# Low parts of some down weights by an accumulating transfer in a two-layer encoder trunk

## The chip, the cores and the metric

The kernel runs on one NeuronCore of a Trainium2 chip. The metric is the device time of one execution in microseconds, as the median of several runs. Every profile here is of one execution. The engines are TensorE (PE in the profile; PEld are its weight loads), VectorE (DVE), ScalarE (ACT), GpSimd (POOL) and SyncE (SP, which issues the DMAs).

## What is computed

The reference is a trunk of two layers on 256 tokens of width 1024, in float32:

```python
for i in range(DEPTH):                                  # DEPTH = 2, ALPHA = (2 * DEPTH) ** 0.25
    x = layer_norm(ALPHA * x + 0.5 * swiglu(x, ffn1_w_gate[i], ffn1_w_up[i], ffn1_w_down[i]), ...)
    proj = x @ (rwkv_w_in[0] if i == 0 else sb_w_in[0])
    mix = rwkv7_mix(...) if i == 0 else stick_breaking_mix(...)
    heads = concatenate([mix, memory_attention(mq, mem_k, mem_v)], axis=-1)
    x = layer_norm(ALPHA * x + heads @ w_out[i], ...)
    x = layer_norm(ALPHA * x + 0.5 * swiglu(x, ffn2_w_gate[i], ffn2_w_up[i], ffn2_w_down[i]), ...)

def swiglu(x, w_gate, w_up, w_down):                    # 1024 x 2816, 1024 x 2816, 2816 x 1024
    return (jax.nn.silu(x @ w_gate) * (x @ w_up)) @ w_down
```

The first layer's mixer is a recurrence over 256 steps (chunks of 64), the second's is a causal attention of its own kind. The weights are read once from device memory; they make up nearly all of the 301 MB that the profile counts as read.

## The kernel before

**Matmuls in three parts.** TensorE multiplies in a reduced float format (float32r). To keep float32 accuracy, each operand is split into a high part, rounded to that format, and a low part, the rest. A product is three matmuls that add up in PSUM (`mm3`, line 664): high by high, high by low, low by high. The tokens are two halves of 128 rows. A matmul has 128 rows of weights as its one operand, 128 tokens as its other, and 512 columns of output.

**Pieces of weights.** `piece` (line 636) handles 128 x 1024 weights at a time, 512 KB. SP loads them into a slot `raw`. ScalarE copies `raw` to a slot `hi`, which rounds it (line 647). VectorE subtracts `hi` from `raw` into a slot `lo` (line 649). There are 10 slots `raw` and 9 each of `hi` and `lo`, 4096 bytes on each partition. A `raw` slot is free for the next load when the subtraction has read it.

**Feed-forward blocks.** `ffn_block` (line 774) does 256 of the 2816 hidden columns: four pieces of gate and up weights (`gu`) and two of down weights (`dn`). For the given halves, it makes 24 matmuls of 512 columns per half into one PSUM bank, then the gating on ScalarE and VectorE, then a transpose, a split into high and low, and 12 matmuls per half with the down weights into the half's accumulators. The down part of a block is put behind the gate and up part of the next one (`blocks`, line 1421).

**Stages.** While one half goes through a layer's mixer, which consists of many short steps on all engines that wait for each other, the other half goes through feed-forward blocks of its own: `solo(1, ...)`, the first blocks of the layer's first feed-forward for half 1, beside the mixer of half 0, and `solo(0, ...)`, the first blocks of the second feed-forward for half 0, beside the mixer of half 1. In layer 0 these are 5 and 9 blocks (`LAGS`, line 47). The remaining blocks serve both halves. A layer norm on VectorE stands between the stages.

**Who sets the order.** The program is first only recorded: each operation becomes an `Op` with a cost (`price`, line 291), its dependencies, and the slots it opens and closes. `order` (line 346) then places the operations one after another on five engine clocks, by the earliest possible start and a priority. SP's loads, the high parts and the low parts each keep a sequence of their own (`in_turn`). `improve` (line 542) repeats that 24 times with priorities from due times that are counted back from the end (`latest`), with a random shake of fixed seed, and keeps the plan with the earliest end. `issue` (line 573) writes the instructions in that order. Each engine's order is thus fixed at build time, all instructions stand under line 599 in the profile, and a change of one cost or one operation changes the order of the whole program. Small copies (`copy`, line 209) may go to ScalarE or VectorE, as the planner finds.

GpSimd does nothing but 14 memsets. All DMAs are issued by SP.

Of the kernel before, what the change touches and what calls it, by code (L numbers as in the profile page):

```python
# [58 lines left out]
BESIDE = (True, False)  # L59


BLK = 16
_LEVELS = [16, 32]

# [66 lines left out]
class Plan:  # L131
# [33 lines left out]
    def slot(self, pool, shape, dtype, tag, name, bufs):  # L165

        handle = bass.PSumTensorHandle if pool.name == "ps" else bass.SBTensorHandle
        tile = handle(name, list(shape), dtype)[:]
        key = pool.name, tag
        self.tag_of[name] = key  # L170
        self.pools[key] = pool
        self.slots[key] = max(bufs, self.slots.get(key, 0))
        self.size[key] = max(int(np.prod(shape[1:])), self.size.get(key, 0))
        return tile

    def region(self, ap):
# [114 lines left out]
    def price(self, o, method, aps, a, k):  # L291
        free = lambda x: int(np.prod([n for _, n in x.ap[1:]])) if len(x.ap) > 1 else 1
        sb = lambda x: x.space != PSUM
        o.func, o.port, o.kb = None, False, 0.0
        outs = [x for x, w in aps if w]
        ins = [x for x, w in aps if not w]
        n = max(free(x) for x, _ in aps)
        far = 0.9 * n * any(len(x.ap) > 1 and x.ap[-1][0] >= 16 and x.ap[-1][1] > 1 for x, _ in aps)
        if o.eng == "PE":
            out, st, mv = a[0], a[1], a[2]  # L300
            cols, m, rows = free(mv), free(st), st.ap[0][1]
            half = lambda x, n: range(x.offset // x.ap[0][0] // 64, (x.offset // x.ap[0][0] + n - 1) // 64 + 1)
            o.mode, o.round = (rows <= 64, m <= 64), st.dtype == F32R
            if method == "transpose":
                took, o.lag = 110.0, 175.0
            elif st.dtype == F32R:
                took, o.lag = max(cols / 2.4, m / 1.2) + 13.3, 180.0
            else:
                took, o.lag = 2 * max(cols / 1.2, m / 1.2 + 4), 200.0
                if rows <= 64 and cols > 128:  # L310
                    took *= 1.25
            o.parts.append((took, [(r, c) for r in half(st, rows) for c in half(out, m)], min(rows, P) / P))
        elif o.eng == "ACT":
            fun = a[2] if len(a) > 2 else k["func"]
            o.func = {AF.Exp: "Exp", AF.Tanh: "Tanh", AF.Sigmoid: "Sigmoid", AF.Ln: "Ln", AF.Silu: "Silu"}.get(fun)
            ptr = sum(isinstance(k.get(x), bass.AP) for x in ("scale", "bias"))
            o.took = 95.0 + 0.845 * n + far + 93.0 * ptr + (92.0 if "accum_out" in k else 0.0)
            o.lag = 95.0
        elif o.eng == "DVE":
            two = sum(sb(x) and free(x) == n for x in ins) > 1  # L320
            big = [x for x in aps if free(x[0]) > 1]
            fast = method in ("tensor_copy", "tensor_scalar") and all(sb(x) for x, _ in aps)
            o.port = two or fast
            ptr = sum(free(x) == 1 and n > 1 for x in ins)
            o.took = 75.0 + n / (1.92 if fast else 0.96) + far + 58.0 * (ptr > 0) * (n > 1)
            if sum(free(x) == 1 for x in ins) > 2:
                o.took += 115.0
            if method == "transpose":
                o.took = 75.0 + n / 0.96 + 60.0
            o.lag = 83.0  # L330
        elif o.eng == "POOL":
            o.port = method != "memset"
            rate = 0.9 if method == "memset" else 2.2 if method in ("tensor_tensor", "tensor_sub", "tensor_mul") else 1.4
            if n <= 70 and method != "tensor_copy":
                rate, base = 1.5, 210.0
            else:
                base = 130.0
            if method == "tensor_copy" and n < 32:
                base = 500.0
            o.took, o.lag = base + rate * n, 78.0  # L340
        else:
            o.kb = max(int(np.prod(x.shape)) for x, w in aps) * 4 / 1024
            o.fine = min(x.shape[-1] for x, w in aps) <= 256
            o.took, o.lag = 400.0, 0.0

    def order(self, given=()):
# [50 lines left out]
        while done < len(ops):  # L397
# [68 lines left out]
            if e == "SP":  # L466
                landed = max(t + LAND + 400.0 * o.fine, landed) + o.kb * 1024 / 330.0
                o.end = landed
            for n in o.opens:
                b = self.buffer[n] = heapq.heappop(free[self.tag_of[n]])[1]  # L470
                self.reuse += [(j, o.i) for j in held.get((self.tag_of[n], b), ())]
                held[self.tag_of[n], b] = set(self.seen[n]["ops"])
# [130 lines left out]
def kernel(ctx, tc, const, x, mem, f1g, f1u, f1d, f2g, f2u, f2d, ln_g, ln_b, w_out, w_mem_kv,  # L603
# [29 lines left out]
        return slice(hf * P, (hf + 1) * P)  # L633


    def piece(shape, *srcs):

        n = int(np.prod(shape))
        hi = new(wp, [P, D], F32R, "hi", "hi", NHI)[:, :n]
        lo = new(wp, [P, D], F32R, "lo", "lo", NLO)[:, :n]  # L640
        raw = new(wp, [P, D], F32, "raw", "raw", NRAW)[:, :n]
        v = lambda t: t.rearrange("p (a b) -> p a b", a=shape[0]) if len(shape) == 2 else t
        m = shape[-1] // len(srcs)
        made = [nc.sync.dma_start(v(raw)[..., i * m:(i + 1) * m], src) for i, src in enumerate(srcs)]
        for o in made:
            nc.in_turn("load", o)
        first = nc.scalar.activation(hi, raw, AF.Copy)
        nc.in_turn("hi", first)
        made.append(nc.vector.tensor_sub(lo, raw, hi.bitcast(F32)))
        nc.in_turn("lo", made[-1])  # L650
        nc.lead.update((o.i, first.i) for o in made + [first])
        return v(hi), v(lo)

# [117 lines left out]
            turn_x(hf)  # L771


    def ffn_block(w, c, halves, beside):
        gv, uv, dv = (m.rearrange("(k p) c -> p k c", p=P) for m in w)
        fs = slice(c * FC, (c + 1) * FC)
        gu = [piece((2, 2 * FC), *(v[:, 2 * g:2 * g + 2, fs] for v in (gv, uv))) for g in range(4)]
        dn = [piece((D,), dv[:, 2 * c + q, :]) for q in range(2)]
        state = {}
        for hf in halves:  # L780
            if todo[hf] == 0:
# [636 lines left out]
        seq += [((i + 0.49) / len(shared), c, range(NHALF)) for i, c in enumerate(shared)]  # L1418
        return [(c, h) for _, c, h in sorted(seq, key=lambda t: t[0])]

    def blocks(w, seq, beside=False):
        waiting = []
        for c, halves in seq:
            hidden = yield from ffn_block(w, c, halves, beside)
            yield from chain(*waiting)
            waiting = hidden()
        yield from chain(*waiting)

    def solo(hf, cs):
        return [(c, [hf]) for c in cs]  # L1430
# [5 lines left out]
    for i in range(DEPTH):  # L1436
        mixer, steps = ((rwkv, RW), (stick, SB))[i % 2]
        last = i == DEPTH - 1
        lag1, lag2 = LAGS[i]
        w = f1g[i], f1u[i], f1d[i]  # L1440
        if i == 0:
            seq = spread((0, range(lag1)), range(lag1, NFC))
            run(blocks(w, seq[:2]))
            nc.in_turn("load", nc.sync.dma_start(cst[:, P:], const[:, P:]))
            run(blocks(w, seq[2:4]))
            rwkv_constants()
            gb = ln_g[i, 0], ln_b[i, 0]
            run(blocks(w, seq[4:]))
        else:
            run(blocks(w, solo(0, range(FIRST))))  # L1450
            gb = ln_g[i, 0], ln_b[i, 0]
            run(blocks(w, spread((0, range(FIRST, lag1)), range(lag1, NFC))))
        norm(0, 2.0 * ALPHA, 4.0 * LN_EPS, gb)
        mixed = []
        run(blocks(w, solo(1, range(HEAD)), BESIDE[0]))
        if i == 0:
            run(memory_kv())
        alternate(chain_steps(mixer(0, mixed)), blocks(w, solo(1, range(HEAD, lag1)), True), steps)
        norm(1, 2.0 * ALPHA, 4.0 * LN_EPS, gb)
        gb = ln_g[i, 1], ln_b[i, 1]  # L1460
        w = f2g[i], f2u[i], f2d[i]
        second = chain_steps(mixer(1, mixed))
        for _ in range(PRE[i]):
            next(second)
        run(chain_steps(mixed_out(0, mixed[0], w_out[i])))
        norm(0, ALPHA, LN_EPS, gb)
        alternate(second, blocks(w, solo(0, range(lag2 - HOLD[i])), True), steps)
        run(chain_steps(mixed_out(1, mixed[1], w_out[i])), blocks(w, solo(0, range(lag2 - HOLD[i], lag2)), BESIDE[1]))
        norm(1, ALPHA, LN_EPS, gb)
        gb = ln_g[i, 2], ln_b[i, 2]  # L1470
        run(blocks(w, spread((1, range(TAIL[i], lag2)), range(lag2, NFC))))
        norm(0, 2.0 * ALPHA, 4.0 * LN_EPS, gb, last)
        run(blocks(w, solo(1, range(TAIL[i]))))
        norm(1, 2.0 * ALPHA, 4.0 * LN_EPS, gb, last)
# [25 lines left out]
```

## Time and profile before

| what | us |
|---|---|
| median of 3 runs | 1103.34 (1101.57 to 1103.51) |
| profiled execution, first to last instruction | 1099.8 |
| TensorE busy | 1062.8 |
| VectorE busy | 928.8 |
| ScalarE busy | 751.6 |
| GpSimd busy | 2.7 |

The profile's page knows the span of the profiled execution alone; the runs' times are 3.5 us above it at the median, which is what lies around the first and the last instruction. Names such as `lo_14r` are slots: the name that the slot's first tile had. One slot serves many pieces after each other. `hi`, `lo` and `raw` are the slots of the weights; `xTh` and `xTl` are the high and low parts of the tokens; `hT` those of the gated hidden values; `ps` are PSUM banks. A matmul of 512 columns stands with a duration of 0.39 us, and the next one starts 0.23 us after it, since matmuls overlap; so TensorE's busy time isn't a measure of how much it could still take. The DMA share is the part of the time in which the 16 DMA engines had packets under way, on average.

### The profile page before, as it was taken

Reading aid. Unit: us, or ns where it says so; the run is one execution under the profiler, and the core shown is the slowest. Engines: PE = TensorE matmul, PEld = TensorE weight load, DVE = VectorE, ACT = ScalarE, POOL = GpSimd, SP = SyncE. Lnnn points to the kernel's source line nnn. Section 1 sums busy time; section 2 is a strip of 40 time slices with the busy share of each in tenths; the row PEclk is TensorE's granted clock in tenths of the full one; section 3 lists DMA queues with packets and bytes.
Section 4 is the critical chain, followed back from the end, with each engine's and each line's share of the span. In section 5 each row is a group of like instructions: output and inputs, shape, how many; then the busy total and the mean of one; then the engine's idle time right before and its main releaser. Section 6 shows DMA issues by size and latency. Waiting matters only on the chain.

```text
span 1099.8 us, 17711 instructions
## 1 busy us (share of the span) xinstructions
PE 1062.8 (97%) x6265; PEld 861.4 (78%) x6265; DVE 928.8 (84%) x1312; ACT 751.6 (68%) x1021; POOL 2.7 (0%) x14
## 2 busy tenths in 40 slices
PE   7999999998799999999999999999999999999996
PEld 6878887876678787778888888888877877888885
DVE  6567677999999999998889965649899989987777
ACT  7466566987369786676668654547898898866652
POOL 0000000000000000000000000000000000000000
PEclk9999999999989999999999999999999999999998
DMA  9499758866679587799989976657987987998781
GB/s 344 149 363 378 262 203 291 295 216 204 190 226 336 179 288 251 256 297 369 323 271 362 352 244 212 206 195 258 392 292 269 349 284 266 376 379 292 264 289 59
DMA packets 212250, 303.30 MB, mean 276 GB/s; under 512 B 13844, under 2 KB 159424, under 8 KB 212162
## 3 DMA queue, kind: packets, MB, share of 16 engines
q1 hardware_dynamic: 212162, 302.18, 80.5%
q8 instruction: 49, 0.80, 0.3%
q14 instruction: 39, 0.32, 0.1%
HBM read 301.08 MB, written 1.05 MB: 275 GB/s over the span
## 4 chain that ended last, share of the span: by engine, by line
PE 79%; DVE 13%; DMA 3%; issue 2%; ACT 2%; SPq 0%; DVEq 0%; ACTq 0%
PE ps_30r L599 25%; PE ps_29r L599 24%; PE ps_26r L599 6%; PE ps_25r L599 6%; PE ps_28r L599 6%; PE ps_27r L599 6%; PE ps_2r L599 3%; PE ps_3r L599 3%; DVE x L599 1%; DMA raw_45r<-in_ffn_w_up_dram 1%; DVE lo_44r L599 1%; DVE lb_498r L599 1%; DMA raw_21r<-in_ffn_w_up_dram 1%; DVE lo_20r L599 1%; DVE lo_17r L599 1%
## 5 line engine op out<-in xcount | busy, mean ns | idle before, releaser
L599 ACT ACTIVATE h_32r<-ps_30r 128x256 f32<-128x256 f32 (+1 forms) x35 | 15.1, 431 | 23.1 <-PE ps_30r L599 23.1
L599 ACT ACTIVATE h_31r<-ps_29r 128x256 f32<-128x256 f32 (+1 forms) x34 | 14.5, 426 | 18.5 <-PE ps_29r L599 18.5
L599 PE MATMUL ps_30r<-hi_22r,xTh 128*128 128x512 f32 x64 | 26.3, 410 | 0.0
L599 PE MATMUL ps_30r<-hi_22r,xTl 128*128 128x512 f32 x64 | 25.0, 391 | 0.0
L599 PE MATMUL ps_30r<-lo_23r,xTh 128*128 128x512 f32 x64 | 25.0, 391 | 0.0
L599 PE MATMUL ps_30r<-hi_10r,xTh 128*128 128x512 f32 (+1 forms) x58 | 23.0, 397 | 0.0
L599 PE MATMUL ps_29r<-hi_16r,xTh 128*128 128x512 f32 x56 | 22.4, 401 | 0.0
L599 PE MATMUL ps_29r<-hi_40r,xTh 128*128 128x512 f32 (+1 forms) x56 | 22.4, 401 | 0.0
L599 PE MATMUL ps_30r<-hi_10r,xTl 128*128 128x512 f32 (+1 forms) x58 | 22.3, 385 | 0.0
L599 PE MATMUL ps_30r<-lo_11r,xTh 128*128 128x512 f32 (+1 forms) x58 | 22.2, 383 | 0.0
L599 PE MATMUL ps_29r<-hi_16r,xTl 128*128 128x512 f32 x56 | 21.9, 391 | 0.0
L599 PE MATMUL ps_29r<-lo_17r,xTh 128*128 128x512 f32 x56 | 21.9, 391 | 0.0
L599 PE MATMUL ps_29r<-hi_40r,xTl 128*128 128x512 f32 (+1 forms) x56 | 21.5, 384 | 0.0
L599 PE MATMUL ps_29r<-lo_41r,xTh 128*128 128x512 f32 (+1 forms) x56 | 21.5, 383 | 0.0
L599 PE MATMUL ps_30r<-hi_13r,xTh 128*128 128x512 f32 x52 | 21.4, 412 | 0.0
L599 PE MATMUL ps_30r<-hi_7r,xTh 128*128 128x512 f32 x52 | 21.2, 408 | 0.0
L599 PE MATMUL ps_30r<-lo_14r,xTh 128*128 128x512 f32 x52 | 20.5, 394 | 0.4 <-DVE lo_14r L599 0.4
L599 PE MATMUL ps_2r<-cst,x 128*128 128x128 f32 x48 | 8.9, 316 | 12.2 <-DVE x L599 6.7
L599 PE MATMUL ps_29r<-lo_44r,xTh 128*128 128x512 f32 x50 | 19.7, 395 | 0.9 <-DVE lo_44r L599 0.8
L599 PE MATMUL ps_30r<-lo_17r,xTh 128*128 128x512 f32 x50 | 19.7, 393 | 0.8 <-DVE lo_17r L599 0.8
L599 PE MATMUL ps_30r<-hi_7r,xTl 128*128 128x512 f32 x52 | 20.4, 392 | 0.0
L599 PE MATMUL ps_30r<-hi_13r,xTl 128*128 128x512 f32 x52 | 20.4, 392 | 0.0
(1923 smaller groups left out, 4044.8 us busy)
## 6 DMA issues: line engine op xcount, KB each, us to landing
raw_45r<-in_ffn_w_down_dram SPq DMA_DIRECT2D x17, 512.0 KB, 4.1
raw_24r<-in_ffn_w_down_dram SPq DMA_DIRECT2D x16, 512.0 KB, 4.6
raw_15r<-in_ffn_w_gate_dram SPq DMA_DIRECT2D x30, 256.0 KB, 4.6
raw_15r<-in_ffn_w_up_dram SPq DMA_DIRECT2D x30, 256.0 KB, 5.6
raw_21r<-in_ffn_w_down_dram SPq DMA_DIRECT2D x15, 512.0 KB, 6.3
raw_39r<-in_ffn_w_gate_dram SPq DMA_DIRECT2D x30, 256.0 KB, 4.8
raw_39r<-in_ffn_w_up_dram SPq DMA_DIRECT2D x30, 256.0 KB, 4.9
raw_42r<-in_ffn_w_down_dram SPq DMA_DIRECT2D x15, 512.0 KB, 5.1
```

What stands on the lines that cost most here:

```text
L599: fn(*[at(x) for x in a], **{n: at(x) for n, x in k.items()})
```

## The change

For some pieces the low part is made in another way: `lo` is not a subtraction on VectorE. ScalarE copies `raw` a second time with a scale of -1 into `lo`, which makes the negated high part there. Then GpSimd issues a DMA from `raw` to `lo` that adds what it reads to what stands in its destination. So `lo` holds `raw` minus the high part when the DMA has landed. TensorE's matmuls on `lo` wait for that DMA, and `raw` is in use until then.

`ADDED` names the pieces: numbers 4 and 5 of a block, the two of the down weights, in the `solo` blocks of layer 0 (first and second feed-forward). That is 2 x (5 + 9) = 28 pieces. In layer 1 there are none. The planner gets a price for the new operation (1 us on GpSimd, 4 us until it has landed, and its bytes on the count of transfers). Slots' sizes are rounded up to 16 elements, 64 bytes.

```diff
+ADDED = (((4, 5), (4, 5)), ((), ()))
+LINE = 16
...
-        self.size[key] = max(int(np.prod(shape[1:])), self.size.get(key, 0))
+        self.size[key] = max(-(-int(np.prod(shape[1:])) // LINE) * LINE, self.size.get(key, 0))
...
+        elif o.eng == "POOL" and method == "dma_start":
+            o.kb = max(int(np.prod(x.shape)) for x, w in aps) * 4 / 1024
+            o.took, o.lag = 1000.0, 4000.0
...
+            elif o.kb:
+                landed += o.kb * 1024 / 330.0
...
-    def piece(shape, *srcs):
+    def piece(shape, *srcs, added=False):
...
-        made.append(nc.vector.tensor_sub(lo, raw, hi.bitcast(F32)))
-        nc.in_turn("lo", made[-1])
+        if added:
+            made.append(nc.scalar.activation(lo, raw, AF.Copy, scale=-1.0))
+            nc.in_turn("lo", made[-1])
+            made.append(nc.gpsimd.dma_start(lo.bitcast(F32), raw, accum_op=ALU.add))
+        else:
+            made.append(nc.vector.tensor_sub(lo, raw, hi.bitcast(F32)))
+            nc.in_turn("lo", made[-1])
...
-        gu = [piece((2, 2 * FC), *(v[:, 2 * g:2 * g + 2, fs] for v in (gv, uv))) for g in range(4)]
-        dn = [piece((D,), dv[:, 2 * c + q, :]) for q in range(2)]
+        gu = [piece((2, 2 * FC), *(v[:, 2 * g:2 * g + 2, fs] for v in (gv, uv)), added=g in added) for g in range(4)]
+        dn = [piece((D,), dv[:, 2 * c + q, :], added=4 + q in added) for q in range(2)]
```

`blocks` hands `ADDED[i][0]` to the `solo` blocks of the first feed-forward and `ADDED[i][1]` to those of the second; the other calls hand over nothing.

More of the change, by code (lines that the diff above doesn't have):

```diff
@@ L771, in norm, with ffn_block @@
             turn_x(hf)
-    def ffn_block(w, c, halves, beside):
+    def ffn_block(w, c, halves, beside, added):
         gv, uv, dv = (m.rearrange("(k p) c -> p k c", p=P) for m in w)
         fs = slice(c * FC, (c + 1) * FC)
-        gu = [piece((2, 2 * FC), *(v[:, 2 * g:2 * g + 2, fs] for v in (gv, uv))) for g in range(4)]
-        dn = [piece((D,), dv[:, 2 * c + q, :]) for q in range(2)]
+        gu = [piece((2, 2 * FC), *(v[:, 2 * g:2 * g + 2, fs] for v in (gv, uv)), added=g in added) for g in range(4)]
+        dn = [piece((D,), dv[:, 2 * c + q, :], added=4 + q in added) for q in range(2)]
         state = {}
@@ L1419, in spread, with blocks @@
         return [(c, h) for _, c, h in sorted(seq, key=lambda t: t[0])]
-    def blocks(w, seq, beside=False):
+    def blocks(w, seq, beside=False, added=()):
         waiting = []
         for c, halves in seq:
-            hidden = yield from ffn_block(w, c, halves, beside)
+            hidden = yield from ffn_block(w, c, halves, beside, added)
             yield from chain(*waiting)
@@ L1454 @@
         mixed = []
-        run(blocks(w, solo(1, range(HEAD)), BESIDE[0]))
+        run(blocks(w, solo(1, range(HEAD)), BESIDE[0], ADDED[i][0]))
         if i == 0:
             run(memory_kv())
-        alternate(chain_steps(mixer(0, mixed)), blocks(w, solo(1, range(HEAD, lag1)), True), steps)
+        alternate(chain_steps(mixer(0, mixed)), blocks(w, solo(1, range(HEAD, lag1)), True, ADDED[i][0]), steps)
         norm(1, 2.0 * ALPHA, 4.0 * LN_EPS, gb)
@@ L1466 @@
         norm(0, ALPHA, LN_EPS, gb)
-        alternate(second, blocks(w, solo(0, range(lag2 - HOLD[i])), True), steps)
-        run(chain_steps(mixed_out(1, mixed[1], w_out[i])), blocks(w, solo(0, range(lag2 - HOLD[i], lag2)), BESIDE[1]))
+        alternate(second, blocks(w, solo(0, range(lag2 - HOLD[i])), True, ADDED[i][1]), steps)
+        run(chain_steps(mixed_out(1, mixed[1], w_out[i])), blocks(w, solo(0, range(lag2 - HOLD[i], lag2)), BESIDE[1], ADDED[i][1]))
         norm(1, ALPHA, LN_EPS, gb)
```

## The prediction

> **What bounds the kernel now.** I read the page first, then the stretches, then the chain inside the first layer. The page's totals, two rows of its slices and its chain by engine:
>
> ```profile
> span 1099.8 us, 17711 instructions
> PE 1062.8 (97%) x6265; PEld 861.4 (78%) x6265; DVE 928.8 (84%) x1312; ACT 751.6 (68%) x1021; POOL 2.7 (0%) x14
> ...
> DVE  6567677999999999998889965649899989987777
> ACT  7466566987369786676668654547898898866652
> ...
> PE 79%; DVE 13%; DMA 3%; issue 2%; ACT 2%; SPq 0%; DVEq 0%; ACTq 0%
> ```
>
> As a whole TensorE is the limit. But busy shares are averages over stages: VectorE's row stands at 9 from the eighth slice to the nineteenth (a slice is 27.5 us), and the chain gives VectorE 13% of the span, 143 us. The stretches (length, then PE, PEld, DVE, ACT, POOL busy, granted clock, DMA share, GB/s) place this:
>
> ```profile
> 158.00:303.00 145.00, 133.98 (x1297) 109.00 (x1295) 136.38 (x242) 100.92 (x164) 0.84 (x4) 0.97 0.73 245
> 303.00:488.00 185.00, 180.05 (x1481) 144.94 (x1482) 182.70 (x310) 138.89 (x202) 0.21 (x1) 0.99 0.79 258
> 200.00:488.00 288.00, 272.45 (x2579) 220.45 (x2578) 282.82 (x505) 208.21 (x320) 1.05 (x5) 0.98 0.74 243
> 488.00:750.00 262.00, 262.00 (x1188) 215.24 (x1187) 198.50 (x244) 157.35 (x196) 0.00 (x0) 1.00 0.83 279
> ```
>
> From 200 to 488 us, the first layer's mixer beside feed-forward blocks, VectorE is busy 282.8 of 288 us (98%), ScalarE 208.2 (72%), GpSimd 1. From 488 on TensorE is busy throughout and VectorE 76%. So VectorE's work has a price in the first layer's mixer stages and none behind them. All 28 pieces that the change touches lie there: 10 with subtractions at 158 to 270 us (five blocks of the first feed-forward), 18 at 336 to 480 us (nine of the second).
>
> **What the change removes.** 28 subtractions on VectorE. One group of such rows, and three rows in a row, which give the pitch:
>
> ```profile
> L599 DVE TENSOR_TENSOR lo_11r<-raw_45r,hi_10r 128x1024 fp32r<-128x1024 f32 x4 | 4.9, 1218 | 3.5 <-ACT hi_10r L599 3.5
> ```
> ```profile
> 409.72 1.22 DVE L599 TENSOR_TENSOR lo_14r<-raw_21r,hi_13r 128x1024 fp32r<-128x1024 f32 x1
> 410.85 1.22 DVE L599 TENSOR_TENSOR lo_23r<-raw_9r,hi_22r 128x1024 fp32r<-128x1024 f32 x1
> 411.99 0.71 DVE L599 STREAM_TRANSPOSE Tt_358r<-Y_369r 128x512 f32<-128x512 f32 x1
> ```
>
> One lasts 1.22 us, but the next operation starts 1.13 us after it: it holds the engine 1.13 us. 28 x 1.13 = 31.6 us of VectorE.
>
> **What it adds on ScalarE.** 28 copies with a scale, next to the plain copy that makes the high part:
>
> ```profile
> 419.00 1.04 ACT L599 ACTIVATE hi_40r<-raw_39r 128x1024 fp32r<-128x1024 f32 x1
> 419.95 1.04 ACT L599 ACTIVATE hi_16r<-raw_15r 128x1024 fp32r<-128x1024 f32 x1
> ```
>
> The pitch is 0.95 us. A constant scale is not shown for this size; the plain copy is the nearest row, so 28 x 0.95 = 26.6 us. ScalarE has 80 us idle in 200 to 488, but not everywhere. I therefore work out the gain by windows, those in which the chain runs over VectorE, where subtractions like these stand on it:
>
> ```profile
> 230.00:271.00 41.00, 37.12 (x348) 28.41 (x347) 40.55 (x75) 32.04 (x61) 0.00 (x0) 0.96 0.64 216
> 346.00:416.00 70.00, 67.33 (x524) 53.48 (x523) 69.78 (x130) 57.91 (x96) 0.21 (x1) 1.00 0.75 242
> 441.00:488.00 47.00, 45.44 (x296) 36.37 (x293) 45.84 (x80) 33.58 (x40) 0.00 (x0) 1.00 0.82 266
> ```
> ```profile
> 237.49 1.14 DVE lo_11r L599
> 238.63 1.14 DVE lo_14r L599
> 239.76 0.68 DVE lo_38r L599
> ```
>
> - 230 to 271 holds six removed subtractions (two are the chain rows above). VectorE falls to 40.55 - 6.78 = 33.8, ScalarE rises to 32.04 + 5.7 = 37.7 and is now the fuller: at most 41 - 37.7 = 3.3 us.
> - 346 to 416 holds eight: VectorE 69.78 - 9.04 = 60.7, ScalarE 57.91 + 7.6 = 65.5: at most 4.5 us.
> - 441 to 488 holds four: VectorE 45.84 - 4.52 = 41.3, ScalarE 33.58 + 3.8 = 37.4: VectorE stays the fuller, 4.5 us.
>
> Together 12.3 us. The other ten (four at 158 to 198, two at 336, four at 422 to 438) lie where the chain runs mostly over matmuls; I count their 11.3 us of VectorE at nothing. What hides them is TensorE; if that cover goes, they are gain as well. This is also a sum over the old windows. The planner places everything anew and may spread ScalarE's load to its idle places, hence the larger rival below.
>
> **The transfer itself.** No row of before shows an accumulating transfer, nor one from GpSimd. Nearest rows: weight loads of the same 512 KB, a load's issue on SP, GpSimd's longest operation:
>
> ```profile
> raw_45r<-in_ffn_w_down_dram SPq DMA_DIRECT2D x17, 512.0 KB, 4.1
> ...
> raw_21r<-in_ffn_w_down_dram SPq DMA_DIRECT2D x15, 512.0 KB, 6.3
> ```
> ```profile
> 411.00 0.37 SPq L599 DMA_DIRECT2D raw_21r<-in_ffn_w_gate_dram  x1
> ```
> ```profile
> L599 POOL MEMSET S_110r<- 128x768 f32 x1 | 0.7, 737 | 0.1
> ```
>
> Bounds: 0.37 + 4.1 = 4.5 us, and, if reading two operands and writing one takes three loads' time, 0.74 + 3 x 6.3 = 19.6 us. I take 0.74 + 6.3 = 7.0, one slow load, because the bytes that land are the same. What waits for it is the first matmul on that low part. How long did the low parts lie ready before? Smallest and largest case of the 28 (the subtraction, then the first matmul that reads its result):
>
> ```profile
> 157.99 1.22 DVE L599 TENSOR_TENSOR lo_14r<-raw_15r,hi_13r 128x1024 fp32r<-128x1024 f32 x1
> ```
> ```profile
> 165.75 0.40 PE L599 MATMUL ps_27r<-lo_14r,hT_35r 128*128 128x512 f32 x1
> ```
> ```profile
> 336.50 1.22 DVE L599 TENSOR_TENSOR lo_17r<-raw_18r,hi_16r 128x1024 fp32r<-128x1024 f32 x1
> ```
> ```profile
> 377.24 0.40 PE L599 MATMUL ps_26r<-lo_17r,hT_833r 128*128 128x512 f32 x1
> ```
>
> 6.5 and 39.5 us; down weights are used only after the next block's gate and up products. In the new order, the matmuls between the last one that the negated copy depends on and the first use add up, by the pitches of before, to 7.0 and 7.3 us in one pair of pieces, to 11 to 15 in eight others, and to over 16 in the rest. That is TensorE's work alone, its idle time comes on top. At 7 us nothing waits. At 19.6 most would.
>
> The transfer also keeps its raw slot until it has landed, and loads wait for raw slots:
>
> ```profile
> SPq L599 <- DVE lo_41r L599: 23.7, 11, 10.3
> ```
> ```profile
> q1 hardware_dynamic: 55616, 82.80, 75.8%
> ```
>
> The second row is DMA between 158 and 488 us: 82.8 MB in 75.8% of the engines' time, so 109 MB would fill it. 28 transfers write 14.7 MB; counted once the stage holds 97.5 MB (89%), counted twice 112 MB, just over. SP's loads stand in order, so one held slot holds all behind it. I take once, and cost it at nothing: ten slots cover it.
>
> **Rounding of slots** changes only the small tiles' sizes and puts one temporary on another offset; raw, high and low slots are 4096 bytes before and after. No row differs by such an offset: zero, either way under 1 us. The counts of table loads, of copies on each engine and of the 870 SP DMAs are the same before and after. The layer-1 order is planned anew too, with nothing added there; that may move a few us in either direction, and I take zero.
>
> **Sum.** 1099.8 - 12.3 = 1087.5 us of span. The median of the runs, 1103.3, is 3.5 us above the span, so 1091.
>
> **Rivals.**
> - *The whole relief arrives.* VectorE is full for 288 us, not only where the chain names it; then all 24 pieces behind 200 us count: 24 x 1.13 = 27.1, giving 1076 (1070 to 1083). For it: the 98%. Against it: ScalarE would be at (208.2 + 22.8) / 261, 89%, with serial mixer steps on it.
> - *The gain is handed back on an engine: no change, 1103.* ScalarE's added copies delay high parts and mixer steps, or VectorE is held while GpSimd prepares a transfer: 28 x 0.37 to 0.74 us is 10 to 21 us on VectorE, the size of the gain. The rows against the latter: GpSimd's few operations here fall beside a full VectorE, whose subtraction still takes 1.22 us; but they are five in 288 us. The Trainium skill, SBUF — State Buffer, section "SBUF: two separate sides", has a rule of this kind: VectorE and GpSimd share one port pair, locked for an instruction at a time, and a transfer issued by GpSimd can starve for its descriptors beside some VectorE operations. No row here shows that. By the rule, the sum would be this rival's 1103.
> - *Late transfers: slower.* The place is the first matmul on a low part, and TensorE's order is fixed, so all behind it waits. Above 7 us the closest pair waits, above 11 to 15 eight more. At 14 us the waits sum to about 7 + 2.9 + 1.7 + 1.6 = 13 us, and the gain is used up: that is the deciding point. At 16 us, about 9 + 4.9 + 3.7 + 3.6 + 2.3 + 2.1 = 26, less 12 gives 1117. For it: DMA at 0.73 to 0.79 before anything is added, and the upper bound of 19.6. Against it: 4.1 to 6.3 for the same bytes.
> - *The change does not do what it says*, the transfers serialised on GpSimd: they are issued on average every 10 us or so, so that is the same case as late transfers.
>
> **Chances.** Forecast 0.56 (own range 1083 to 1100), whole relief 0.16, no change 0.14, slower 0.14. A measurement of this kernel tells about 0.2% (2.2 us) from no change. So faster 0.72, same 0.14, slower 0.14. The range 1076 to 1110 leaves about half of the whole-relief case below it and most of the far end of the slower one above: it reaches no further since the bounds of the transfer count only beyond 14 us.
>
> **What would show it.** VectorE's busy total down by about 32 us and its share in the mixer stages below 95%; ScalarE's up by 27; transfers that land in 5 to 8 us; no waits of TensorE on them beyond 1 us; the end of the first layer's second mixer stage, now at 488 us, earlier by about 12. Wrong would be: low-part matmuls waiting for transfers, subtractions longer than 1.22 us, SP waiting for transfers and TensorE for loads, or layer 1 longer by more than a few us from its new order.

## The result and the profile after

The changed kernel takes 1110.53 us (median of four runs, 1109.31 to 1111.25) against 1102.78 us: the ratio is 1.0069, with a 95% interval of 1.0057 to 1.0081. It is slower by 0.7%, and the forecast was faster by 1.1%. The profiled execution took 1110.0 us, with a span of 1108.2.

The page of the kernel after: totals, three rows of the slices, the two large queues, and the chain by engine.

```profile
span 1108.2 us, 17779 instructions
PE 1068.7 (96%) x6265; PEld 863.3 (78%) x6265; DVE 899.2 (81%) x1284; ACT 772.9 (70%) x1049; POOL 27.0 (2%) x42
...
DVE  6577675899999996878879965549989989987776
ACT  6466565988469897677757655536897898866652
...
DMA  9499878969879999999989987667987987999881
...
q1 hardware_dynamic: 212162, 302.18, 79.4%
q0 software_dynamic: 4032, 14.68, 6.9%
...
PE 77%; DMA 10%; DVE 5%; ACT 3%; issue 3%; SPq 1%; DVEq 0%; POOL 0%; ACTq 0%; POOLq 0%
```

VectorE did lose its work: 928.8 - 899.2 = 29.6 us less, of the 31.6 that were counted. ScalarE rose by 21.3. In the chain VectorE falls from 13% to 5% of the span, but DMA rises from 3% to 10%, 111 us: the end is now set more often by data that has not arrived, loads and the transfers alike (their parts follow with e6). The same stretches as before, and the three windows from which the gain was worked out (length, then PE, PEld, DVE, ACT, POOL busy, granted clock, DMA share, GB/s):

```profile
158.00:303.00 145.00, 136.95 (x1300) 111.07 (x1299) 123.22 (x212) 109.27 (x173) 8.59 (x13) 0.98 0.88 274
303.00:488.00 185.00, 176.48 (x1470) 142.08 (x1467) 164.13 (x308) 149.28 (x215) 16.13 (x21) 0.98 0.98 299
```
```profile
230.00:271.00 41.00, 38.74 (x365) 30.20 (x365) 39.07 (x80) 33.70 (x62) 3.64 (x5) 0.96 0.77 221
346.00:416.00 70.00, 69.33 (x543) 56.36 (x542) 66.79 (x131) 65.48 (x112) 7.09 (x9) 1.00 0.99 294
441.00:488.00 47.00, 44.48 (x321) 35.45 (x320) 37.43 (x71) 34.23 (x42) 3.94 (x5) 1.00 1.06 333
```

The column to read is the last but one. The DMA share goes from 0.73 to 0.88 and from 0.79 to 0.98; from 441 to 488 us it is over 1, so some records of packets overlap, and a share near 1 is only roughly full; by this measure the engines had hardly any free time there. The transfers by queue between 158 and 488 us, the stretch of the row that the forecast quoted (packets, MB, share of 16 engines):

```profile
q1 hardware_dynamic: 53330, 80.21, 69.9%
q0 software_dynamic: 3955, 14.43, 22.9%
```

A megabyte of weights costs 69.9 / 80.21 = 0.87% of the stretch, a megabyte of accumulating transfers 22.9 / 14.43 = 1.59%: 1.8 times as much. 22.9% of 330 us are 75.6 us of all 16 engines; a transfer of 0.524 MB has 2.7 us of them. The loads of the same stretch fell from 82.80 to 80.21 MB: they are behind those of before.

Where did the time come from? The layer norms mark the stages. Their rows in both kernels, before and then after:

```profile
152.23 0.21 DVE L599 BATCH_NORM_AGGREGATE mv_284r<-st_283r 128x2 f32<-128x12 f32 x1
...
293.24 0.21 DVE L599 BATCH_NORM_AGGREGATE mv_628r<-st_627r 128x2 f32<-128x12 f32 x1
...
477.82 0.21 DVE L599 BATCH_NORM_AGGREGATE mv_628r<-st_627r 128x2 f32<-128x12 f32 x1
...
571.15 0.21 DVE L599 BATCH_NORM_AGGREGATE mv_284r<-st_283r 128x2 f32<-128x12 f32 x1
```
```profile
152.72 0.21 DVE L606 BATCH_NORM_AGGREGATE mv_284r<-st_283r 128x2 f32<-128x12 f32 x1
...
298.14 0.21 DVE L606 BATCH_NORM_AGGREGATE mv_628r<-st_627r 128x2 f32<-128x12 f32 x1
...
483.41 0.21 DVE L606 BATCH_NORM_AGGREGATE mv_628r<-st_627r 128x2 f32<-128x12 f32 x1
...
578.98 0.20 DVE L606 BATCH_NORM_AGGREGATE mv_284r<-st_283r 128x2 f32<-128x12 f32 x1
```

From one start to the next, with the experiments told below (same rows of their traces):

| stage, us | before | after | e5: no transfer | e4: short transfer | e6: bystander | e9: two short ones |
|---|---|---|---|---|---|---|
| first mixer stage (152 to 293) | 141.0 | 145.4 | 139.3 | 139.3 | 143.4 | 156.5 |
| memory, second mixer stage (293 to 478) | 184.6 | 185.3 | 182.5 | 183.4 | 188.0 | 183.1 |
| to the last norm of layer 0 (478 to 571) | 93.3 | 95.6 | 91.7 | 91.7 | 95.3 | 99.0 |
| layer 1, to the end | 528.6 | 529.2 | 529.2 | 529.6 | 529.3 | 529.2 |

Of the 8.4 us by which the span is longer, 7.3 lie in these three stages of layer 0, 4.4 + 0.7 + 2.2; layer 1's new order costs 0.6 us, and 0.5 lie ahead of the table.

### The profile page after: what moved, and what is told of

Its sections match the earlier page's. It is cut to its first block, busy times and chain, and to the rows that moved or that the text cites. A ratio compares the mean times of both kernels' runs of the same rounds, so it can differ in the third digit from the quotient of the medians.

```text
span 1108.2 us, 17779 instructions
## 1 busy us (share of the span) xinstructions
PE 1068.7 (96%) x6265; PEld 863.3 (78%) x6265; DVE 899.2 (81%) x1284; ACT 772.9 (70%) x1049; POOL 27.0 (2%) x42
## 4 chain that ended last, share of the span: by engine, by line
PE 77%; DMA 10%; DVE 5%; ACT 3%; issue 3%; SPq 1%; DVEq 0%; POOL 0%; ACTq 0%; POOLq 0%
PE ps_30r L606 24%; PE ps_29r L606 24%; PE ps_25r L606 6%; PE ps_27r L606 6%; PE ps_26r L606 6%; PE ps_28r L606 6%; PE ps_3r L606 3%; PE ps_2r L606 2%; DMA T_368r<-in_rwkv_lnx_g_dram 1%; DMA raw_24r<-in_ffn_w_up_dram 1%; DMA lo_44r<-raw_9r 1%; DMA lo_8r<-raw_18r 1%; DMA lo_17r<-raw_21r 1%; DMA lo_14r<-raw_24r 1%; DMA lo_17r<-raw_39r 1%
## 5 line engine op out<-in xcount | busy, mean ns | idle before, releaser
L606 PE MATMUL ps_29r<-hi_10r,xTh 128*128 128x512 f32 x58 | 23.8, 410 | 0.0
L606 PE MATMUL ps_30r<-hi_37r,xTh 128*128 128x512 f32 (+1 forms) x58 | 23.1, 397 | 0.0
L606 PE MATMUL ps_30r<-lo_8r,xTh 128*128 128x512 f32 x58 | 22.9, 396 | 0.0
L606 PE MATMUL ps_29r<-lo_11r,xTh 128*128 128x512 f32 x58 | 22.7, 391 | 0.0
L606 PE MATMUL ps_29r<-hi_10r,xTl 128*128 128x512 f32 x58 | 22.7, 391 | 0.0
L606 PE MATMUL ps_30r<-hi_16r,xTh 128*128 128x512 f32 x56 | 22.6, 403 | 0.0
L606 PE MATMUL ps_30r<-lo_38r,xTh 128*128 128x512 f32 (+1 forms) x58 | 22.2, 383 | 0.3 <-issue 0.3
L606 PE MATMUL ps_30r<-hi_37r,xTl 128*128 128x512 f32 (+1 forms) x58 | 22.2, 383 | 0.0
L606 PE MATMUL ps_29r<-hi_16r,xTh 128*128 128x512 f32 (+1 forms) x54 | 21.9, 406 | 0.0
L606 PE MATMUL ps_30r<-hi_16r,xTl 128*128 128x512 f32 x56 | 21.9, 391 | 0.0
L606 PE MATMUL ps_29r<-hi_37r,xTh 128*128 128x512 f32 x50 | 20.8, 415 | 0.0
L606 PE MATMUL ps_29r<-hi_16r,xTl 128*128 128x512 f32 (+1 forms) x54 | 20.7, 383 | 0.0
```

The lines of the kernel that those rows point to most:

```text
L606: fn(*[at(x) for x in a], **{n: at(x) for n, x in k.items()})
```

## The experiments

Two theories stood at the start. **Slots**: the transfer keeps its raw slot for 8 us, SP's loads stand in order behind it, so weights come late. **DMA time**: the transfers take so much of the DMA engines that the loads are late whatever the slots do. Beside them: late low parts, ScalarE, and the planner's order. In most kernels the plan is that of the kernel after and only what is emitted for some operations differs (`nc.swap[...]`, looked up at the place where an operation is issued), so that the order does not move with the experiment.

**The subtraction in the new order.** e1 emits VectorE's subtraction at the place of the transfer, and no negated copy.

```diff
+            nc.swap[made[-2].i] = []
+            nc.swap[made[-1].i] = [(nc.real.vector.tensor_sub, (lo, raw, hi.bitcast(F32)), {})]
```

> The changed kernel's instruction order, but the 28 low parts are made by VectorE's subtraction at the place of the transfer: no second copy on ScalarE, no transfer. Theory 'slots' (the transfers keep raw slots 5 to 12 us and SP's loads stand behind them) and theory 'engines' (the transfers' 22% of the DMA engines' time slows the loads): VectorE has its 31.6 us back, but no load is late any more, so 1100 to 1107, below the changed kernel's 1110.5. Theory 'order' (the newly planned order is the worse one, whatever makes the low parts): 1110 or more, since nothing but VectorE's work is added to that order. Theory 'ScalarE' (the added copies delay it): 1100 to 1107 as well.

Measured: 1115.77 us, ratio 1.0121 (1.0106 to 1.0136). That is where 'order' had put it, and above what the other theories expected. In the new order, the new way is 5 us better than the old. The new order is made for a VectorE with less to do, so this does not price the order by itself; e5 and e4 below keep this order and come out faster than the kernel before. What e1 shows is that the relief is real.

**The new way in the old order.** e2 keeps the kernel before, its plan too, and emits copy and transfer where each of the 28 subtractions stood.

```diff
+            nc.swap[made[-1].i] = [(nc.real.scalar.activation, (lo, raw, AF.Copy), dict(scale=-1.0)),
+                                   (nc.real.gpsimd.dma_start, (lo.bitcast(F32), raw), dict(accum_op=ALU.add))]
```

> The order of before, unchanged on every engine, but in each of the 28 places of the subtraction ScalarE makes the negated copy and GpSimd issues the transfer. 'Slots' and 'engines': slower than before, 1106 to 1115, with SP waiting for transfers. 'Order': faster than before, 1091 to 1100, since VectorE is relieved and nothing else moved. 'ScalarE': slower, with TensorE or VectorE waiting for high parts rather than for loads.

Measured: 1147.49 us, ratio 1.041 (1.0392 to 1.0428), far above the 1106 to 1115 that were expected. Two rows of SP's queue's waits between 300 and 520 us (in total, times, longest):

```profile
SPq L601 <- DMA lo_20r<-raw_18r: 10.9, 1, 10.9
...
SPq L601 <- DMA lo_8r<-raw_42r: 10.2, 1, 10.2
```

A plan that knows nothing of the transfers loses 45 us. That low parts are wanted and slots are counted on sooner there is the likely reason; how the 45 us divide between the two was not tried.

**The slots.** In e3 the transfer reads the weights from device memory instead of from `raw`, so `raw` is free after the two copies; all else is as after.

```diff
+            nc.swap[made[-1].i] = [(nc.real.gpsimd.dma_start, (lo, srcs[0].bitcast(F32R)), dict(accum_op=ALU.add))]
```

> The changed kernel's order, with the same transfers, but what they add is read from the weights in device memory and not from the raw slot, so that the slot is free when ScalarE has copied it twice. The DMA engines move as many bytes. 'Slots': 1097 to 1104, the loads come earlier by some 8 us in 28 places. 'Engines': 1110 or more, as the engines' work is the same and device memory is read for it as well. 'Order' and 'ScalarE': 1110.

Measured: 1110.83 us, ratio 1.0069 (1.0049 to 1.0088): no change against after, though SP no longer waits for any transfer. In the kernel after, SP's waits on transfers sum to 75.1 us between 150 and 520 us, and the largest row is:

```profile
SPq L606 <- DMA lo_44r<-raw_21r: 8.8, 1, 8.8
```

The engine time is the same: the software queue has 20.7% of that stretch in e3 and 20.8% after. The transfers read 14.7 MB more from device memory here, which might cost something of its own and hide a gain; e5 and e4 do without that.

**No transfer.** e5 leaves the transfers out.

```diff
+            nc.swap[made[-1].i] = []
```

> The changed kernel's order with the second copy on ScalarE but with no transfers: the 28 low parts hold the negated high part alone, so this part of the computation is left out. 'Slots' and 'engines': 1092 to 1102, all of the relief of VectorE and no late load. 'Order' and 'ScalarE': 1108 to 1111, as the order and ScalarE's work are those of the changed kernel.

Measured: 1097.96 us, ratio 0.9959 (0.9943 to 0.9974). So all that the relief of VectorE is worth in this order is 4.8 us by the medians, and the transfers cost 1110.53 - 1097.96 = 12.6. The page's chain of e5, and its windows:

```profile
PE 87%; DVE 6%; ACT 3%; DMA 2%; issue 1%; SPq 0%; DVEq 0%; ACTq 0%
```
```profile
230.00:271.00 41.00, 38.08 (x363) 29.15 (x362) 39.02 (x80) 35.42 (x68) 0.20 (x1) 1.00 0.61 216
346.00:416.00 70.00, 69.14 (x578) 55.80 (x578) 65.22 (x124) 65.51 (x108) 0.20 (x1) 1.00 0.74 249
441.00:488.00 47.00, 45.22 (x269) 36.51 (x269) 41.48 (x70) 38.08 (x46) 0.00 (x0) 1.00 0.84 275
```

VectorE is relieved (65.2 of 70 us in the second window), ScalarE stands at the 65.5 that were forecast, and TensorE is the fullest of the three, at 69.1. The chain agrees: VectorE's 13% became 6%, and TensorE's 79% became 87%.

**All waits, no bytes.** e4 is the kernel after, with a transfer of 16 of the 1024 columns.

```diff
+            nc.swap[made[-1].i] = [(nc.real.gpsimd.dma_start, (lo.bitcast(F32)[:, :16], raw[:, :16]), dict(accum_op=ALU.add))]
```

> The changed kernel's order and all its waits, but a transfer adds only the first 16 of 1024 columns; the other columns of the 28 low parts hold the negated high part, so that part of the computation is left out. Its engine time goes nearly to nothing, its landing to about 3 us. 'Engines': 1097 to 1101, that of the kernel without transfers (1098.0). 'Slots': a slot is still held until landing, 3 us in place of 8, so 1101 to 1105. 'Late transfers': 1098.

Measured: 1098.47 us, ratio 0.9957 (0.9941 to 0.9972), the same as without a transfer. From the end of the negated copy to the landing it takes 4.5 us at the median here, 8.5 in the kernel after. Issue, wait, slot, and the same number of packets: together they cost nothing when it lands in 4.5 us. The software queue's row between 150 and 520 us shows what is missing:

```profile
q0 software_dynamic: 4032, 0.23, 1.9%
```

**Bytes for which nobody waits.** e6 takes e4 and issues behind each short transfer a plain copy of 256 rows of 4 KB from device memory to a scratch in device memory, for which nobody waits.

```diff
+    aside, scratch = [], tc.nc.dram_tensor("aside", (28, P, 2, D + 16), F32, kind="Internal").ap()
...
+            to = scratch[len(aside) - 1][:, :, :D]
+            nc.swap[made[-1].i] = [(nc.real.gpsimd.dma_start, (lo.bitcast(F32)[:, :16], raw[:, :16]), dict(accum_op=ALU.add))] + [(nc.real.gpsimd.dma_start, (to, srcs[0].unsqueeze(1).to_broadcast((P, 2, D))), {})]
```

> As the short transfer, and behind each one GpSimd issues a plain copy of 256 rows of 4 KB from weights in device memory to a scratch area there. Nobody waits for it and it holds no slot; it only takes the DMA engines' time, as much as the full transfer if one row takes 170 ns (the full transfer: 128 rows of 341 ns). The low parts are as in the short one. 'Engines': 1106 to 1112. 'Slots': that of the short transfer, 1098 to 1103.

Measured: 1110.27 us, ratio 1.0067 (1.0049 to 1.0084): the time of the kernel after, to 0.3 us. The software queue between 150 and 520 us, the page's chain, and the stretches of e6:

```profile
q0 software_dynamic: 11648, 29.59, 22.2%
```
```profile
PE 78%; DMA 9%; DVE 7%; ACT 3%; issue 2%; SPq 0%; DVEq 0%; ACTq 0%
```
```profile
158.00:303.00 145.00, 136.84 (x1300) 110.97 (x1298) 125.14 (x221) 108.64 (x173) 15.29 (x22) 0.98 0.89 315
303.00:488.00 185.00, 176.94 (x1462) 142.16 (x1462) 161.90 (x296) 149.19 (x215) 29.53 (x39) 0.98 0.97 343
```

The copies were sized to the engine time of the transfers: 22.2 - 1.9 = 20.3% of 370 us, 75 us, against 20.8% in the same stretch of the kernel after, 77 us. Shares (0.89, 0.97), TensorE's and ScalarE's busy times and the page's chain come out close to the kernel after. Engine time for which nobody waits is enough for a loss of this size. That the totals agree to 0.3 us is partly luck: against e4 the three stages of layer 0 lose 4.1, 4.6 and 3.6 us in e6, but 6.1, 1.9 and 3.9 in the kernel after.

Two things differ beside. The copies move 29 MB through device memory, which the transfers don't; but the loads' packets did not become dearer by it, 69.6% for 80.46 MB between 158 and 488 us against 69.9% for 80.21 after. And the short transfers are slower beside the copies: from negated copy to landing they take 6.5 us at the median (2.9 to 11.3), and SP's waits on them sum to 65.3 us, against 37.5 in e4. So e6 by itself does not rule out the slots; e3 does, with the same time and no such wait. In e6 in turn no wait of TensorE for a transfer shows. The chain inside layer 0, the longest pieces of after and then of e6 (start, us, what):

```profile
427.42 11.41 DMA lo_44r<-raw_9r
480.66 11.20 DMA lo_8r<-raw_18r
158.95 10.68 DMA lo_17r<-raw_21r
```
```profile
244.21 12.55 DMA raw_9r<-in_ffn_w_up_dram
479.65 12.05 DMA raw_45r<-in_ffn_w_down_dram
399.04 11.97 DMA raw_15r<-in_ffn_w_up_dram
```

Between 150 and 580 us the chain runs 50.8 us over transfers and 48.4 over loads in the kernel after, 18.3 and 60.3 in e3, 6.3 and 83.4 in e6, 12.6 and 18.2 in e4. The three slow kernels lose the same time by different waits; what they share is the engine time. How much of the loss of the kernel after goes by late transfers and how much by late loads is not separated.

That the loads are late shows at the engine that takes them first. The waits of ScalarE's high parts for loads between 150 and 520 us, the largest of before and the three largest of after:

```profile
ACT hi_19r L599 <- DMA raw_42r<-in_ffn_w_up_dram: 1.7, 1, 1.7
```
```profile
ACT hi_37r L606 <- DMA raw_45r<-in_rwkv_w_in_dram: 2.9, 1, 2.9
ACT hi_13r L606 <- DMA raw_45r<-in_w_out_dram: 2.5, 1, 2.5
...
ACT hi_40r L606 <- DMA raw_21r<-in_ffn_w_down_dram: 2.1, 1, 2.1
```

All such rows of ScalarE sum to 2.7 us before, 21.8 after, 2.3 in e5, 5.2 in e4, 20.0 in e3 and 19.3 in e6: among the five kernels with the relief, the slow three are those in which these waits are long.

**Held longer.** To price lateness without bytes, e7 emits three of e4's short transfers after each other, and e9 two.

```diff
+            nc.swap[made[-1].i] = 2 * [(nc.real.gpsimd.dma_start, (lo.bitcast(F32)[:, :16], raw[:, :16]), dict(accum_op=ALU.add))]
```

> As the short transfer, but three of them in a chain on the same 16 columns, each issued when the one before has landed: the raw slot and the low part are held about as long as by the full transfer (7 to 9 us), with next to no engine time. The 28 low parts are not what they should be. 'Slots': 1107 to 1111, the changed kernel's time. 'Engines': 1098 to 1102.

Measured: 1174.95 us, ratio 1.0653 (1.0631 to 1.0675). From copy to landing it took 18.3 us at the median, twice what was aimed at, so this prices another case.

> As the chain of three short transfers, but two: the chain of three held the slots 18.3 us (median, from the negated copy to the landing) where the full transfer holds them 8.5 and one short transfer 4.5. Two should hold 9 to 12, with next to no engine time. 'Engines' alone: 1098 to 1101. 'Slots' as a cause beside it: 1104 to 1120, since holding for 18 us gave 1175 and for 4.5 us 1098.

Measured: 1120.68 us, ratio 1.0145 (1.0112 to 1.0178), at 11.2 us from copy to landing (6.8 to 16.2). TensorE's largest waits on transfers between 150 and 520 us:

```profile
PE ps_27r L607 <- DMA lo_17r<-raw_21r: 6.4, 2, 3.4
PE ps_27r L607 <- DMA lo_11r<-raw_18r: 4.2, 1, 4.2
```

Lateness thus has a price as well, and a steep one: nothing at 4.5 us, 22 us at 11.2 (against e4), with almost no engine time; by the table above, 17.3 of them in the first mixer stage and 7.3 in the stage before the last norm. The kernel after, at 8.5, stands between them, and lateness of 8.5 us without the bytes was not tried. Its own such row is small, and e6 reaches the same time without it:

```profile
PE ps_27r L606 <- DMA lo_17r<-raw_21r: 2.5, 1, 2.5
```

**Whether ScalarE took over.** e14 leaves the transfers out and cuts the negated copies to 16 columns.

```diff
+            nc.swap[made[-1].i] = []
+            nc.swap[made[-2].i] = [(nc.real.scalar.activation, (lo[:, :16], raw[:, :16], AF.Copy), dict(scale=-1.0))]
```

> The changed kernel's order without transfers, and with the negated copy cut to 16 of 1024 columns, so that ScalarE is relieved of 28 x 0.8 us too; the 28 low parts are otherwise left as they stand in the slot, a part of the computation that is left out. 'ScalarE took over': 1089 to 1094, well below the 1098.0 of the kernel with full copies. 'TensorE took over': 1096 to 1098, no further gain.

Measured: 1097.27 us, ratio 0.9943 (0.9927 to 0.996). The window at 346 us, to compare with that of e5:

```profile
346.00:416.00 70.00, 69.30 (x578) 56.15 (x577) 65.55 (x124) 59.99 (x109) 0.20 (x1) 1.00 0.74 248
```

ScalarE has 5.5 us less to do there, and the time stays. ScalarE was not the next limit.

**Rounding, and the draw of the plan.** The planner tries orders from a seed. e8 is the kernel before with slots rounded to 64 bytes and its order kept; e12 is before, and e13 after, with another seed.

```diff
-        self.size[key] = max(int(np.prod(shape[1:])), self.size.get(key, 0))
+        self.size[key] = max(-(-int(np.prod(shape[1:])) // 16) * 16, self.size.get(key, 0))
```
```diff
-SEED = 144
+SEED = 145
```

> The kernel before with slots rounded to 64 bytes and nothing else; the order of all instructions is the same. All theories: no difference, 1101.5 to 1104.

> The kernel before with the planner's random seed 145 in place of 144: the same operations, another order. 'Order' as the cause: 1108 or more, the order of before being a lucky one. If the plans differ little: 1100 to 1106, and the difference between before and after is not one of draws.

> The changed kernel with the planner's random seed 145 in place of 144. 'Engines': 1107 to 1114, again above the kernel before, since the transfers' engine time does not depend on the draw. 'Order': below 1104.

Measured: e8 1102.86 us, ratio 1.0001 (0.9992 to 1.001); e12 1103.19, ratio 1.0005 (0.9995 to 1.0015); e13 1111.98, ratio 1.0078 (1.0062 to 1.0094). The rounding is not the cause, and with one other seed on each side the difference is as large, so a lucky or unlucky plan is not either.

**Fewer transfers, and a better price.** e11 makes only the first feed-forward's 10 pieces in the new way, e15 one piece of each block (14); e10 keeps all 28 and tells the planner 0.9 and 7.5 us and twice the bytes. All three are planned anew.

```diff
-ADDED = (((4, 5), (4, 5)), ((), ()))
+ADDED = (((4, 5), ()), ((), ()))
```
```diff
-ADDED = (((4, 5), (4, 5)), ((), ()))
+ADDED = (((4,), (4,)), ((), ()))
```
```diff
-            o.took, o.lag = 1000.0, 4000.0
+            o.took, o.lag = 900.0, 7500.0
...
-                landed += o.kb * 1024 / 330.0
+                landed = max(t, landed) + 2.0 * o.kb * 1024 / 330.0
```

> The changed kernel with only the 10 pieces of the first feed-forward by transfer; the order is planned anew. Before, the DMA share was 0.73 in that stage and 0.79 in the other. 'Engines': 10 transfers of 2.6 us of all engines against 145 us with a quarter free, so there is room: 1098 to 1104. 'Order': anything within some 10 us, as each plan is another draw.

> The changed kernel with one piece of each block in place of two by transfer, 14 in all, planned anew. 'Engines': half of the engine time, 37 us of some 84 free, and half of the relief: 1102 to 1107.

> The changed kernel, but the planner is told what the transfer was measured to cost: 0.9 us on GpSimd, 7.5 us to its landing in place of 4, and twice its bytes on the count of transfers. The order is planned anew. 'Slots' (a transfer that lands later than planned holds up the loads): 1098 to 1106. 'Engines': the stage has no room for the transfers' engine time wherever they stand, so 1106 to 1112.

Measured: e11 1105.15 us, ratio 1.002 (1.0009 to 1.0031); e15 1106.62, ratio 1.0035 (1.0023 to 1.0047); e10 1117.86, ratio 1.0137 (1.0122 to 1.0152). Ten pieces cost 2.4 us, 14 cost 4.1 and 28 cost 7.8, between 0.24 and 0.29 us each: none of the three numbers pays. No version that computes all of it was faster than the kernel before.

Two of these miss what was expected of 'engines'. e11 was to find room in its stage (1098 to 1104), at a share of 0.73 before. It is there that it loses: its first mixer stage takes 143.4 us against 141.0, at a share of 0.87 between 158 and 303 us. So time that is free on average did not make the transfers free. e10 was to stay within 1112. Its two mixer stages are in fact 4.5 us shorter than before (141.4 and 179.7 us); all that it loses comes behind them, up to the last norm of layer 0, where it takes 111.1 us against 93.3. This stage, before and then in e10:

```profile
478.00:571.00 93.00, 91.80 (x417) 75.14 (x416) 79.62 (x96) 62.81 (x76) 0.00 (x0) 1.00 0.94 324
```
```profile
474.00:585.00 111.00, 104.30 (x456) 84.84 (x457) 89.32 (x104) 72.41 (x91) 2.58 (x3) 0.97 1.00 335
```

Before, it already stood at a DMA share of 0.94, with 30.0 MB of loads; in e10 it has 35.0 MB, and the transfers take 10.1% of it. This suggests that loads which were put off beside the mixer are paid for in the next stage, which has no room; why the planner chose so with the better price stays open.

## Why the prediction was wrong

**The step that failed first** is in the part on the transfer: DMA was costed "at nothing: ten slots cover it", with the bytes counted once. The prediction had both numbers: 109 MB would fill the stage, 97.5 with bytes counted once, 112 with bytes counted twice. The measured price was 1.8 times a load's, so by the same sum 82.8 + 14.7 x 1.8 = 109 MB: full. In the trace of after, the two queues take 69.9 + 22.9 = 92.8% of the stretch. Its error was also to think of slots as the cover: with the same ten slots the loads are late throughout, and ScalarE's waits for them go from 2.7 to 21.8 us. This term was 0 and measures 12.6 us.

**The step that failed second** is the gain by windows: 12.3 us forecast, 4.8 measured in e5. The caps compared VectorE with ScalarE, and the third number stood in the same rows: TensorE at 37.12 of 41, 67.33 of 70 and 45.44 of 47 us left 3.9, 2.7 and 1.6 us, 8.2 together, where 3.3, 4.5 and 4.5 were counted. The least of the caps in each window gives 3.3 + 2.7 + 1.6 = 7.6, which is nearer though still high. e14 shows that ScalarE was not what held, and e5's chain names TensorE. That TensorE's idle time is the cap is argued and not shown: the window at 346 us holds 578 matmuls in e5 and 524 before, at 69.14 and 67.33 us busy, so busy time is no strict measure of the work done. By stage, e5 gains 1.7 us in the first mixer stage, where 3.3 were forecast, 2.1 in the second, where 9.0 were, and 1.6 behind it, where none were. What took the rest was not tried.

Both are taken against e5, so 4.8 gained and 12.6 lost make up the 7.75 us of the result by construction; the sum is no check of the two causes. A smaller point: the 3.5 us between span and median are not all outside the span. Where a run's time and span are both on record, 1.8 us lie outside (1110.0 against 1108.2 after); the rest is that the profiled run of before was a quick one, 1101.6 against the median of 1103.3. VectorE's row stands at 9 up to the eighteenth slice, not the nineteenth.

**Right**: the subtraction's 1.13 us (29.6 us less on VectorE, of 31.6 counted) and the copy's pitch, which two rows of ScalarE after show as 0.95:

```profile
409.91 1.06 ACT L606 ACTIVATE lo_23r<-raw_45r 128x1024 fp32r<-128x1024 f32 x1
410.86 1.05 ACT L606 ACTIVATE lo_17r<-raw_42r 128x1024 fp32r<-128x1024 f32 x1
```

ScalarE's 65.5 us at 346 to 416 came to 65.48. Rounding came to 0, layer 1's order to 0.6. The transfer's landing was taken as 7.0 us; a typical group, the shortest and the longest of the 28 (KB each, median us from issue to landing):

```profile
lo_17r<-raw_21r POOLq DMA_DIRECT2D x2, 512.0 KB, 8.8
...
lo_20r<-raw_12r POOLq DMA_DIRECT2D x1, 512.0 KB, 5.0
...
lo_17r<-raw_42r POOLq DMA_DIRECT2D x1, 512.0 KB, 11.6
```

The median of all 28 is 8.2, within the bounds but above the 5 to 8 that were named as the sign of success. TensorE's waits on transfers sum to some 3 us; one of 2.5 us, in the first mixer stage, is longer than the 1 us that was named.

**The rivals.** The whole relief (1076) falls with e5: without any transfer, the time is still 1098. *Handed back on an engine* falls too: ScalarE by e14, and VectorE held by GpSimd by the subtractions that are left. The 11 that ran beside an issuing instruction of GpSimd took 1218 ns on average, the other 501 took 1221. The group that was shown before (1218 ns then):

```profile
L606 DVE TENSOR_TENSOR lo_11r<-raw_45r,hi_10r 128x1024 fp32r<-128x1024 f32 x4 | 4.9, 1216 | 0.0
```

So the lock on the shared port pair of which the Trainium skill tells (SBUF — State Buffer, "SBUF: two separate sides") did not show up in VectorE's durations here. Whether descriptors came late beside VectorE can't be told apart from their queueing behind loads. *Late transfers* had the sign right, and e9 shows that the mechanism is there at 11 us, as "above 11 to 15 eight more" had it; but the place it named, the first matmul on a low part, is not needed for the loss, since in e6 no wait of TensorE for a transfer shows. The tell that the prediction named, "SP waiting for transfers", is in the trace and misleads: e3 takes those 75.1 us of waits away and gains nothing.

## What to carry to other kernels

Before work is handed to DMA, price it in engine time as a share of the stage that it falls into, with a dearer packet than a load's until one is measured: here shares of 0.73 and 0.79 left room for a quarter to a fifth, the transfers asked for 22.9%, and even ten of them, in a stage that then stood at 0.87, did not pay. Look at the next stage too: one that stands at 0.94 has little room for what was put off. When an engine is relieved, compare the gain with the fullest of all the others in the same window, TensorE's own busy row included. And a wait that shows up in the trace is a candidate and no cause: one kernel that takes the wait away, and one that adds the resource's load with as few new waits as can be, told them apart together, and neither would have alone.

## What was not expected of the hardware

- An accumulating transfer within SBUF cost 1.8 times the DMA time of a load from device memory with the same bytes: in the trace a packet of 4 KB has 341 ns on average, that of a load 183 ns in the same kernel and 195 ns in the kernel before (158 to 488 us), and that of e6's copies within device memory 167 ns. e3's transfers, which read device memory, have 340 ns, so where they read made no difference.
- From the end of the negated copy, a transfer of 16 columns landed after 4.5 us and one of 1024 columns after 8.5 us, both beside loads.
- Small transfers that wait for each other add up: two took 11.2 us from copy to landing, three 18.3 us. Part of this is a queue: GpSimd issues in order, so in e9 the first transfer to `lo_23r`, whose copy ended at 246.6 us, was issued at 250.7, after that to `lo_38r` had landed at 249.8.
- The DMA share of a window can stand above 1 (1.06 at 441 to 488 us), so a value near 1 does not say exactly how much time is left.
